# Where the input tiles of a recurrent block start in on-chip memory: shifting them by multiples of 4, 16 and 32 bytes

## The chip, the core and the metric

The kernel runs on one core of a Trainium2 chip. The metric is the device time in microseconds (us) of one execution; lower is better. The kernel before has a median of 2161.11 us over three runs (2160.96 to 2161.13).

## The reference

A two-layer trunk on 1024 tokens of width 1024, in float32: layer 0 mixes tokens with an RG-LRU recurrent block, layer 1 with stick-breaking attention, and each is followed by a SwiGLU feed-forward network (FFN) of width 2816. Norms stand before every part and at the end. The part that matters here is the recurrent block:

```python
def rg_lru_block(x, w_in, b_in, conv_w, conv_b, gate_w, gate_b, lam, w_out, b_out):
    u = jnp.einsum("bsd,de->bse", x, w_in) + b_in          # input product, 1024 -> 2048
    gate_branch, rec = u[..., :LRU_WIDTH], u[..., LRU_WIDTH:]
    rec = causal_depthwise_conv(rec, conv_w, conv_b)
    ...                                                     # block-diagonal gates r and i from rec
    _, h = lax.associative_scan(_linear_recurrence_combine, (a, b), axis=1)
    y = jax.nn.gelu(gate_branch, approximate=True) * h
    return jnp.einsum("bse,ed->bsd", y, w_out) + b_out      # output product, 1024 -> 1024
```

## The kernel before

All activations lie transposed: 128 channels on the partitions, tokens along the free axis, in two halves of 512 tokens (n = 0 left, n = 1 right). A width of 1024 is eight such tiles, d or k = 0 to 7.

A float32 product is made from three matmuls of a reduced type (fp32r). Each operand is split into a high tile and a low tile, its remainder, and `mm3` (L638 to L641) adds high x high, low x high and high x low in one bank of PSUM. The weights are the stationary operand (128 x 128, loaded by LDWEIGHTS); the input is the moving operand (128 x 512). The three matmuls of one k are on L639 (weights high, input high), L640 (weights high, input low) and L641 (weights low, input high). One column of a product, 128 output channels of one half, is eight k, so 24 matmuls.

The moving tiles of the recurrent block are `xh` (high) and `xl` (low), eight of each, a left and a right half for each: 32 tiles of 512 elements, 2048 bytes in each partition. They come from one pool, `xp`, opened by `open_x` (L570). Three pieces of work read them, and a fourth lies between:

- the first four columns of the input product, whose weights `fh` and `fl` are in a pool `sp` of their own (names a_ps<-xh,fh and so on), 192 matmuls, with four small ones for the norm's sums among them;
- the other twelve columns of the input product, 576 matmuls, whose weights `whi` and `wlo` come from a ring of weight tiles of 1024 elements (pools `wp` and `wq`, at the other end of the memory);
- the gates do not read them: their moving tiles `rh` and `rl` are in a pool `lp`, 192 matmuls (g_ps), weights from the ring;
- the output product, 16 columns, 384 matmuls (ob_ps), after the block's result y has been written into the same xh and xl; weights from the ring.

ScalarE writes xh (L758 from the input, L982 from y) and VectorE writes xl as the difference (L761, L983). After the output product the pool is closed, and tiles of the FFN (`vh`, `vl`) are put in its place. From there on other moving tiles are used.

What sets the order: the first part is written out by hand; a planner orders the rest of the recurrent block from its own table of costs, and the FFN again is written out by hand. Every engine works through its own queue; SP's queue issues most of the transfers. Neither the planner nor any of the lists reads an address.

Pools are filled from two ends of the memory of a partition: xp, lp and sp from the low end, one after the other, the ring from the high end. Start addresses of the kernel before, as the program is built, in bytes within a partition:

| tiles | first start | start modulo 256 |
|---|---|---|
| xh, xl (xp, 32 tiles) | 19328 | 128, all |
| fh, fl (sp) | 85248 | 0, all |
| rh, rl (lp) | | 128, all |
| whi, wlo (wp, wq) | 204672 and above | 128, all |
| vh, vl of the FFN | | 128, all |

One k of a weight tile is 512 bytes of it, so within a weight tile the start modulo 256 does not change with k.

Of the kernel before, what the change touches and what calls it, by code (L numbers as in the profile page):

```python
# [10 lines left out]
F32R = mybir.dt.float32r  # L11
# [6 lines left out]
P = 128  # L18
S = 1024
D = 1024  # L20
ND = D // P
NT = S // P
NB = 512
NH = S // NB
# [480 lines left out]
def trunk(  # L505
# [61 lines left out]
    xh, xl = [None] * ND, [None] * ND  # L567
    xstk = ExitStack()

    def open_x():  # L570
        xp = xstk.enter_context(tc.tile_pool(name="xp", bufs=1, reuse_waits="tile"))
        for x_, nm in ((xh, "xh"), (xl, "xl")):
            for d in range(ND):
                x_[d] = [xp.tile([P, NB], F32R, name=f"{nm}{d}_{n}") for n in range(NH)]
    rcol = cp.tile([P, NT], F32, name="rcol")
    minus = cp.tile([P, 112], F32R, name="minus")
    fresh = tiny[:, 60:61]
# [120 lines left out]
    def gain(h, d, n):  # L698
        g = (vc[:, V_FIN : V_FIN + ND], tiny[:, 32 : 32 + ND])[n]
        nc.scalar.activation(h[d][n], h[d][n], AF.Copy, scale=g[:, d : d + 1])  # L700

    open_x()
    hd = [[dp.tile([P, NB], F32, name=f"hd{d}_{n}") for n in range(NH)] for d in range(ND)]
    hstk = ExitStack()
# [1569 lines left out]
```

## Time and profile before

| | us |
|---|---|
| median of the runs | 2161.11 |
| span of the profiled execution, first to last instruction | 2159.4 |
| what lies around the span (2161.11 - 2159.4) | 1.7 |
| TensorE busy | 2148.2 |
| VectorE busy | 1715.8 |
| ScalarE busy | 1099.4 |
| input product with fh, fl | first 52 |
| rest of the input product, and gates | 52 to 226 |
| output product | 226 to 313 |

The profile gives for every instruction its start and its duration. Matmuls are pipelined, so the duration of one (389 ns) contains the time in which the next is running already; what counts for the time is the distance between the starts of one and the next. A group's row names the line, the engine, the operation, and output <- inputs by the names in the program. Times are in us from the start of the span.

### The profile page before, as it was taken

The numbers are of one execution on the slowest core, as the hardware profiler recorded it, in microseconds if no ns is written. First come the engines' busy times: TensorE is split into PE (matmuls) and PEld (weight loads), VectorE is DVE, ScalarE is ACT, GpSimd is POOL, SyncE is SP. The second block draws the span as 40 slices with busy tenths as digits, with TensorE's granted clock in tenths as the row PEclk, the third lists the DMA queues.
The fourth block names the chain that finished last, engine by engine and source line by source line (L and its number), as shares of the span: only waits on it lengthen the run. The fifth ranks groups of instructions, "written<-read, shape, count | busy, mean of one in ns | idle before, by whom it ended". The sixth has DMA issues, their size and how long they took to land.

```text
span 2159.4 us, 27027 instructions
## 1 busy us (share of the span) xinstructions
PE 2148.2 (99%) x9954; PEld 1781.6 (83%) x9954; DVE 1715.8 (79%) x2416; ACT 1099.4 (51%) x1793; POOL 29.2 (1%) x40
## 2 busy tenths in 40 slices
PE   9999999999999999999999999999999999999998
PEld 7888888888888888878888888888888888888887
DVE  8978678667777887888888888877967777787887
ACT  6677445344444544565555555544534444454555
POOL 0000020000000000000000000002000000000000
PEclk9999999999999999999999999999999999999999
DMA  4111312344444764444333334532133444467452
GB/s 177 39 49 49 127 39 84 100 139 146 133 160 136 276 198 122 147 141 103 100 97 96 101 88 107 167 139 95 59 117 125 145 140 151 141 233 243 130 161 86
DMA packets 133316, 274.61 MB, mean 127 GB/s; under 512 B 15296, under 2 KB 23872, under 8 KB 133184
## 3 DMA queue, kind: packets, MB, share of 16 engines
q1 hardware_dynamic: 132768, 272.36, 39.6%
q8 instruction: 78, 1.28, 0.2%
q10 hardware_dynamic: 416, 0.52, 0.1%
q14 instruction: 54, 0.44, 0.1%
HBM read 176.88 MB, written 70.78 MB: 115 GB/s over the span
## 4 chain that ended last, share of the span: by engine, by line
PE 96%; DVE 2%; ACT 1%; issue 0%; DMA 0%; POOL 0%; SPq 0%; DVEq 0%; ACTq 0%; POOLq 0%
PE p_ps L641 18%; PE p_ps L639 18%; PE p_ps L640 18%; PE qk_ps L639 4%; PE qk_ps L641 4%; PE qk_ps L640 4%; PE z_ps L2073 3%; PE av_ps L2121 3%; PE wt_ps L2104 3%; PE a_ps L640 3%; PE a_ps L641 3%; PE a_ps L639 3%; PE ob_ps L639 2%; PE ob_ps L640 2%; PE ob_ps L641 2%; PE g_ps L641 1%
## 5 line engine op out<-in xcount | busy, mean ns | idle before, releaser
L639 PE MATMUL p_ps<-vh,wbh 128*128 128x512 f32 x524 | 204.0, 389 | 1.2 <-ACT ta L1738 1.2
L641 PE MATMUL p_ps<-vh,wal 128*128 128x512 f32 x524 | 204.2, 390 | 0.5 <-DVE wal L1133 0.3
L641 PE MATMUL p_ps<-vh,wbl 128*128 128x512 f32 x524 | 204.1, 390 | 0.0
L641 PE MATMUL p_ps<-vh,wcl 128*128 128x512 f32 x524 | 204.0, 389 | 0.0
L639 PE MATMUL p_ps<-vh,wch 128*128 128x512 f32 x524 | 203.9, 389 | 0.0
L640 PE MATMUL p_ps<-vl,wah 128*128 128x512 f32 x524 | 203.9, 389 | 0.0
L640 PE MATMUL p_ps<-vl,wbh 128*128 128x512 f32 x524 | 203.9, 389 | 0.0
L639 PE MATMUL p_ps<-vh,wah 128*128 128x512 f32 x524 | 203.9, 389 | 0.0
L640 PE MATMUL p_ps<-vl,wch 128*128 128x512 f32 x524 | 203.8, 389 | 0.0
L1138 ACT CAST wbh<-sb 128x1024 fp32r<-128x1024 f32 (+2 forms) x69 | 69.8, 1011 | 191.3 <-DVE sb L1122 191.3
L2085 ACT ACTIVATE F<-z_ps 128x512 f32<-128x512 f32 (+3 forms) x188 | 92.1, 490 | 97.6 <-PE z_ps L2073 95.8
L2109 ACT CAST th<-wt_ps 128x512 fp32r<-128x512 f32 x192 | 92.3, 481 | 84.4 <-PE wt_ps L2104 78.1
L2092 DVE TENSOR_TENSOR_SCAN F<-F,unit 128x128 f32<-128x128 f32 (+3 forms) x128 | 104.9, 821 | 33.4 <-ACT F L2085 32.2
L2113 DVE TENSOR_TENSOR tl<-wt_ps,th 128x512 fp32r<-128x512 f32 x192 | 104.9, 546 | 16.6 <-ACT th L2109 16.5
L641 PEld LDWEIGHTS p_ps<-vh,wal 128*128 128x128 f32 x524 | 98.4, 188 | 22.0 <-DVE wal L1133 1.8
L639 PEld LDWEIGHTS p_ps<-vh,wbh 128*128 128x128 f32 x524 | 98.4, 188 | 21.9 <-ACT ta L1738 1.6
L641 PEld LDWEIGHTS p_ps<-vh,wbl 128*128 128x128 f32 x524 | 98.4, 188 | 21.2 <-DVE wbl L1142 0.8
L641 PEld LDWEIGHTS p_ps<-vh,wcl 128*128 128x128 f32 x524 | 98.4, 188 | 20.7 <-DVE wcl L1152 0.4
L640 PEld LDWEIGHTS p_ps<-vl,wbh 128*128 128x128 f32 x524 | 98.4, 188 | 20.5
L640 PEld LDWEIGHTS p_ps<-vl,wah 128*128 128x128 f32 x524 | 98.4, 188 | 20.5
L639 PEld LDWEIGHTS p_ps<-vh,wch 128*128 128x128 f32 x524 | 98.4, 188 | 20.5
L640 PEld LDWEIGHTS p_ps<-vl,wch 128*128 128x128 f32 x524 | 98.4, 188 | 20.5
(436 smaller groups left out, 5496.4 us busy)
## 6 DMA issues: line engine op xcount, KB each, us to landing
raw<-in_ffn_w_in SPq DMA_DIRECT2D x88, 512.0 KB, 3.6
vl<-pd SPq DMA_DIRECT2D x128, 256.0 KB, 3.5
pd<-U SPq DMA_DIRECT2D x90, 256.0 KB, 2.3
raw<-in_ffn_w_out SPq DMA_DIRECT2D x28, 512.0 KB, 4.1
raw<-in_attn_w_qkv SPq DMA_DIRECT2D x24, 512.0 KB, 3.8
kh<-qh SPq DMA_DIRECT2D x64, 128.0 KB, 2.3
kl<-ql SPq DMA_DIRECT2D x64, 128.0 KB, 2.3
acc<-pd SPq DMA_DIRECT2D x28, 256.0 KB, 2.6
```

The costliest lines, as they stand in the source:

```text
L639: nc.tensor.matmul(ps, lhsT=wh, rhs=mh, start=first, stop=False, **kw)
L640: nc.tensor.matmul(ps, lhsT=wh, rhs=ml, start=False, stop=False, **kw)
L641: nc.tensor.matmul(ps, lhsT=wl, rhs=mh, start=False, stop=last, **kw)
L1138: nc.scalar.copy(self.full(self.wb), self.full(self.sb))
L2073: nc.tensor.matmul(ps[:, 0:n], lhsT=lhsT, rhs=rhs, start=i == 0, stop=i == 1)
L2085: nc.scalar.activation(F, Z.pop(c)[:, 0:n], AF.Sigmoid, scale=-SC)
L2092: V.tensor_tensor_scan(rev, rev, unit[:, NB - n :][:, ::-1], 0.0, op0=ALU.mult, op1=ALU.add)
L2104: nc.tensor.transpose(tp[:, c : c + P], F[:, (kb % 4) * P : (kb % 4 + 1) * P], ident)
L2109: nc.scalar.copy(WH[u][:, c:], TP[u][:, c:])
L2113: V.tensor_sub(WL[u][:, c:], TP.pop(u)[:, c:], f32(WH[u])[:, c:])
L2121: nc.tensor.matmul(ps[:, c:], lhsT=VV[q][:, kb, hx], rhs=t.pop(u)[:, c:], start=kb == 4 * G and i == 0, stop=kb == 3 and i == 1,)
```

## The change

The right halves of xh and xl are taken out of tiles that are 8 elements (32 bytes) longer, and start a few elements into them: 4 elements (16 bytes) for every xh, and 1, 2, 3, 5, 6, 7, 1, 2 elements (4 to 28 bytes) for the eight xl. The left halves start at the start of their tiles. Since each pair is 32 bytes longer, all later tiles of the pool start later too.

```diff
     def open_x():
         xp = xstk.enter_context(tc.tile_pool(name="xp", bufs=1, reuse_waits="tile"))
-        for x_, nm in ((xh, "xh"), (xl, "xl")):
-            for d in range(ND):
-                x_[d] = [xp.tile([P, NB], F32R, name=f"{nm}{d}_{n}") for n in range(NH)]
+        for x_, nm, shifts in ((xh, "xh", (4,) * ND), (xl, "xl", (1, 2, 3, 5, 6, 7, 1, 2))):
+            for d, shift in enumerate(shifts):
+                left = xp.tile([P, NB], F32R, name=f"{nm}{d}_0")
+                x_[d] = [left, xp.tile([P, NB + 8], F32R, name=f"{nm}{d}_1")[:, shift : shift + NB]]
```

In the built program, by start addresses before and after:

| tiles | start after, against before |
|---|---|
| left half of pair p (p = 0 to 7: xh0 to xh7; 8 to 15: xl0 to xl7) | + 32 p bytes |
| right half of an xh | + 32 p + 16 bytes |
| right half of an xl | + 32 p + 4, 8, 12, 20, 24, 28, 4, 8 bytes |
| sp and lp (fh, fl, rh, rl and others) | + 512 bytes |
| the ring, the FFN's tiles, attention's tiles | the same |

The instructions, their shapes and their order on each engine are the same. Of the waits two differ: among the loads of the residual tiles on SP's queue (L714) the wait for VectorE stands at a load three places later, and one of ScalarE's writes of a vh tile of the FFN (L1054), which now lies over two of the old tiles, waits for TensorE.

## The prediction

> **What bounds the kernel now.** I read the page first: busy shares, then the chain of waits.
>
> ```profile
> PE 2148.2 (99%) x9954; PEld 1781.6 (83%) x9954; DVE 1715.8 (79%) x2416; ACT 1099.4 (51%) x1793; POOL 29.2 (1%) x40
> PE 96%; DVE 2%; ACT 1%; issue 0%; DMA 0%; POOL 0%; SPq 0%; DVEq 0%; ACTq 0%; POOLq 0%
> ```
>
> TensorE is busy 99% of the span and holds 96% of the chain, so what changes the pace of its matmuls changes the time one for one. The busy time of one matmul (389 ns) is no pace, since matmuls overlap; the pace is the distance from one start to the next, which I call the step. It comes from first and last starts of the groups that read xh and xl (tile view; the times are first and last start):
>
> ```profile
> L639 PE MATMUL a_ps<-xh,whi x192: 389/389/389, 52.5 to 225.9; 128*128 128x512 f32 x192
> L639 PE MATMUL ob_ps<-xh,whi x128: 389/389/389, 226.6 to 312.9; 128*128 128x512 f32 x128
> L641 PE MATMUL a_ps<-xh,fl x64: 390/394/545, 7.1 to 52.2; 128*128 128x512 f32 x64
> ```
>
> Each group is every third matmul. ob_ps: 127 x 3 = 381 steps in 86.3 us, 226.5 ns each. a_ps from whi: 191 x 3, and the 192 gate matmuls (g_ps) between them, 765 steps in 173.4 us, 226.7 ns. So 960 matmuls on xh and xl (576 of a_ps, 384 of ob_ps) step at 226.7 ns. The 192 first ones, whose weights are fh and fl, take longer: 63 x 3 steps and 4 of the norm sums in 45.1 us, 233.7 ns, a little of it from the start. In order of time, in the middle of that stretch and where it ends:
>
> ```profile
> 19.64 0.40 PE L640 MATMUL a_ps<-xl,fh 128*128 128x512 f32 x1
> 19.88 0.39 PE L641 MATMUL a_ps<-xh,fl 128*128 128x512 f32 x1
> 20.11 0.40 PE L639 MATMUL a_ps<-xh,fh 128*128 128x512 f32 x1
> 20.34 0.39 PE L640 MATMUL a_ps<-xl,fh 128*128 128x512 f32 x1
> ...
> 21.97 0.40 PE L641 MATMUL a_ps<-xh,fl 128*128 128x512 f32 x1
> ...
> 51.76 0.40 PE L639 MATMUL a_ps<-xh,fh 128*128 128x512 f32 x1
> 52.00 0.40 PE L640 MATMUL a_ps<-xl,fh 128*128 128x512 f32 x1
> 52.24 0.40 PE L641 MATMUL a_ps<-xh,fl 128*128 128x512 f32 x1
> 52.47 0.39 PE L639 MATMUL a_ps<-xh,whi 128*128 128x512 f32 x1
> 52.70 0.40 PE L640 MATMUL a_ps<-xl,whi 128*128 128x512 f32 x1
> 52.93 0.39 PE L641 MATMUL a_ps<-xh,wlo 128*128 128x512 f32 x1
> 53.16 0.39 PE L639 MATMUL a_ps<-xh,whi 128*128 128x512 f32 x1
> ...
> 55.88 0.39 PE L639 MATMUL a_ps<-xh,whi 128*128 128x512 f32 x1
> ```
>
> 19.64 to 21.97 is ten steps, 233 ns each. The same xh and xl stand on both sides of 52.47; what changes is the weight tile. From 53.16 to 55.88 are twelve steps, 226.7 ns, and so it stays. In the built programs the xp tiles before the change start 128 bytes past a multiple of 256, the ring tiles (whi, wlo) too; fh and fl start on a multiple of 256. Relative start of weights to moving tile, modulo 256: 0 in the quick stretch, 128 in the slow one.
>
> Two other causes for the slow stretch were open: its loads, and that the kernel is only starting.
>
> ```profile
> 12.00:32.00 20.00, 20.00 (x87) 1.00 0.68 259
> 32.00:52.00 20.00, 20.00 (x87) 1.00 0.12 41
> 60.00:100.00 40.00, 40.00 (x178) 1.00 0.12 40
> ```
>
> These are stretches with TensorE's busy time and matmuls, granted clock, DMA share and GB/s. The count in 20 us is 87 under 259 GB/s and under 41 GB/s; 60 to 100 us, with the DMA share of the second, has 178 in 40 us. The clock is full in all. So the load is not it, and it lasts until the weight tile changes.
>
> The quick step is a state that matmuls fall into, not one that each has for itself. After a wait for a weight tile, in an FFN:
>
> ```profile
> 333.33 0.50 PE L641 MATMUL p_ps<-vh,wal 128*128 128x512 f32 x1
> 333.66 0.40 PE L639 MATMUL p_ps<-vh,wah 128*128 128x512 f32 x1
> 333.90 0.40 PE L640 MATMUL p_ps<-vl,wah 128*128 128x512 f32 x1
> 334.13 0.40 PE L641 MATMUL p_ps<-vh,wal 128*128 128x512 f32 x1
> 334.37 0.39 PE L639 MATMUL p_ps<-vh,wah 128*128 128x512 f32 x1
> 334.59 0.39 PE L640 MATMUL p_ps<-vl,wah 128*128 128x512 f32 x1
> ...
> 335.75 0.39 PE L639 MATMUL p_ps<-vh,wah 128*128 128x512 f32 x1
> ...
> 337.79 0.39 PE L639 MATMUL p_ps<-vh,wah 128*128 128x512 f32 x1
> ```
>
> 333.66 to 335.75 is nine uneven steps (240, 230, 240, 220 ns as rounded), 232 ns on average; from 335.75 nine steps in 2.04 us, 226.7 ns. At 52.47 three steps were enough. With fh and fl nearly 200 steps were not. I take it that the relative start decides whether the even step exists.
>
> **The change part by part.** No instruction is added, removed or moved; sizes and order on every engine are the same. Three things differ.
>
> (1) Starts. Each right tile is 32 bytes longer, so the p-th pair (p = 0 to 15: xh0 to xh7, xl0 to xl7) starts 32p bytes later. Left tiles go to multiples of 32 relative to the ring, right tiles of xh a further 16, right tiles of xl a further 4 to 28. Of 16 left tiles two keep relative start 0 modulo 256 (xh0, xl0) and two get 128 (xh4, xl4); right tiles keep it nowhere. Along a column of eight k the relative start changes after every third matmul. An even step that needs relative start 0 finds it for three matmuls of 24 on the left, where nine were needed after 333.66, and for none on the right. So I let all 960 matmuls lose it. The trace has no step at the new relative starts; the nearest rows are the unsettled ones, 232 ns (5.3 dearer), and those at 128, 233 ns (6.3 dearer). Bounds: 0, if only 128 and what is near it matters, and the longest step seen in the slow stretch, 240 ns as rounded (19.64 to 19.88), 13 dearer. I take 5.5, nearer to the unsettled rows, since changing starts never leave it one pattern. 960 x 5.5 ns = 5.3 us (0 to 12.8).
>
> (2) The gate matmuls (g_ps, 192) have tiles 512 bytes later, so their relative start is the same. They come in some eight stretches between columns and need three to nine steps to settle: 8 x 6 x 5.5 ns = 0.3 us (0 to 1.1, were all 192 unsettled). The FFN after 313 us settles once: under 0.1.
>
> (3) The first 192: fh and fl move by 512 bytes, so their starts against xh and xl become mixed, not 128 throughout. If they settled at 226.7 they would gain 192 x 6.3 = 1.2 us; at 240 they would lose 1.3. Unsettled before and after, I take 0.
>
> ScalarE and VectorE write the shifted tiles.
>
> ```profile
> L758 ACT ACTIVATE xh<-xr,vc x16: 717/722/734, 5.0 to 22.4; 128x512 fp32r<-128x512 f32 x16
> L761 DVE SCALAR_TENSOR_TENSOR xl<-xr,vc,xh x16: 745/747/752, 5.7 to 25.4; 128x512 fp32r<-128x512 f32 x16
> L983 DVE TENSOR_TENSOR xl<-y,xh x16: 665/686/694, 221.5 to 235.7; 128x512 fp32r<-128x512 f32 x16
> ```
>
> Their prices at odd starts are not in the trace; half of each 16 are on right tiles. TensorE covers them: of the first product, columns of the right half start after 96 matmuls, 96 x 233 ns = 22 us after 7.1, so at 29, while the last xl is written by 26.2. In the output product k = 6 and 7 come after 72 matmuls, at 226.6 + 72 x 0.2267 = 242.9, and the last xl ends at 236.4. Without that cover a doubling would cost about 8 x 0.7 us each time; here 0. Two waits move too. On SP's queue the wait for VectorE ahead of the residual loads stands three transfers later, so three loads may go earlier. On ScalarE the first write of a vh6 tile gets a wait for a matmul of the output product:
>
> ```profile
> L1054 ACT ACTIVATE vh<-h,vc x4: 710/713/722, 324.2 to 326.0; 128x512 fp32r<-128x512 f32 x4
> ```
>
> That write is at 324 us or later, the output product is over by 313.5: 0. Behind it on ScalarE are casts for the same FFN, with TensorE supplied from the products before.
>
> The Trainium skill ("SBUF — State Buffer", on cachelines of 16 bytes) has each crossing to a new line cost something. A right xl tile off that grid touches 129 lines, not 128; as an estimate from that page and the step above, 226.7 / 128 = 1.8 ns on 192 matmuls, 0.3 us. The sum would be 0.3 by that alone, and no run here shows it yet.
>
> Sum: 5.3 + 0.3 + 0 = +5.6 us on a span of 2159.4, so 2165.0. The median of the runs, 2161.1, lies 1.7 above that span; the prediction is 2166.7.
>
> **The rivals.**
>
> A (forecast): the even step is lost on xh and xl. Own range from 960 x 3.3 = 3.2 us (all at the 230 ns of the three settling steps from 52.47 to 53.16) to 1152 x 6.3 = 7.3 us: 2164.3 to 2168.4. For it: the switch at 52.47 and nothing else that switches there.
>
> B: nothing happens, 2161.1; not slower. Mechanism: the moving tile and the next weights are read without touching each other, and the first 52 us are slow through what is special to fh and fl themselves (their own start, their narrower tile), which keeps its place modulo 256. For it: only one pool shows the slow pattern. Against: the unsettled steps in the FFN look like it with other tiles. It decides if 60 to 313 us stays at 226.7. The Trainium skill speaks for B: "TensorE: Matmul & The Clock Gate" (Step-by-step) says TensorE has two independent read ports, so that loading the next weights takes nothing from the running matmul; by that rule the time would stay. The step that depends on the weight tile at 52.47 speaks against it.
>
> C: part of it. Only right tiles, off the 32-byte grid, or only those near 128, lose the even step: half of 960, 480 x 5.5 = 2.6 us, 2163.8. For it: no row shows a relative start of 32 or 64.
>
> D: odd starts cost by themselves, an extra piece per read beside the lost step: all 960 at 240 ns or so, 12.8 us, with (2) 2174; half of that extra, 2170. For it only that 240 ns steps occur.
>
> E: faster. A new even step shorter than 226.7. The step from 334.37 to 334.59 shows that 220 ns as rounded occurs; kept for 960 it would give 960 x 6.7 = 6.4 us, 2154.7. Against: it occurs singly and is followed by 230.
>
> **How the numbers follow.** A 0.52, C 0.20, B 0.15, D 0.08, E 0.05. A measurement here tells 0.2% (4.3 us) from no change, so slower begins at 2165.4: some 85% of A (0.45), D (0.08), a little of C (0.02): 0.55. Within: the rest of A, nearly all of C, B, part of E: 0.42. Faster: 0.03. The range goes from 2160.9, which takes in B and C, to 2171.5, which leaves out most of E and about half of D.
>
> **What would show it.** Starts of xh groups: ob_ps's first and last 86.3 us apart now, 88.4 by A, 87.4 by C, unchanged by B. If the columns of the left half stay at 226.7 and only those of the right half lose it, the 32-byte steps were harmless. If the first 52 us grow or shrink by more than 1 us, (3) was wrong. Idle time of TensorE between 52 and 313 us, none now, would mean that a write or a wait was not covered. Wrong altogether if the added time lies after 340 us, where no start changes.

## The result, and the profile after

The changed kernel takes 2166.36 us (median of 10 runs, 2166.07 to 2167.77). The kernel before, on the same chip and between the same runs, takes 2161.19 us (10 runs, 2160.96 to 2161.87). The ratio is 1.0024, with a 95% interval of 1.0014 to 1.0033: slower by 5.2 us. The forecast was 2166.7. The profiled executions stand at spans of 2163.9 and 2159.4 us, 4.5 apart.

The page of the changed kernel, TensorE's share and the chain of waits:

```profile
PE 2152.1 (99%) x9954; PEld 1780.5 (82%) x9954; DVE 1715.6 (79%) x2416; ACT 1098.3 (51%) x1793; POOL 29.0 (1%) x40
PE 95%; DVE 3%; ACT 1%; issue 1%; DMA 0%; SPq 0%; DVEq 0%; ACTq 0%
```

Nothing here tells that anything is wrong: TensorE is busy 99% as before. The kernel got slower without a new wait of any size. The waits of TensorE in the changed kernel begin with these two, one at the start of the kernel and one at 943 us, where the first FFN ends and the attention has not begun:

```profile
PE a_ps L775 <- POOL ident masks.py:199: 1.5, 1, 1.5
PE p_ps L640 <- ACT ta L1739: 1.2, 1, 1.2
```

The same view of the changed kernel between 52 and 313 us has no entry. The loss shows where the first and last starts of a group are read. The tile view of xh in the changed kernel, after the counts the shortest, median and longest duration in ns, then first and last start in us (its lines are one higher than before):

```profile
L640 PE MATMUL a_ps<-xh,whi x192: 387/394/399, 52.1 to 228.4; 128*128 128x512 f32 x192
L640 PE MATMUL ob_ps<-xh,whi x128: 387/395/421, 229.1 to 317.5; 128*128 128x512 f32 x128
L642 PE MATMUL a_ps<-xh,fl x64: 387/393/401, 6.8 to 51.9; 128*128 128x512 f32 x64
L762 DVE SCALAR_TENSOR_TENSOR xl<-xr,vc,xh x16: 745/747/750, 5.7 to 25.6; 128x512 fp32r<-128x512 f32 x16
L984 DVE TENSOR_TENSOR xl<-y,xh x16: 665/684/696, 223.7 to 238.2; 128x512 fp32r<-128x512 f32 x16
```

- a_ps from the ring, with the gates between: 176.3 us from first to last start against 173.4 before, so 2.9 more.
- ob_ps: 88.4 us against 86.3, so 2.1 more: 381 steps of 232.0 ns, where they were 226.5.
- a_ps with fh and fl: 45.1 us, as before.
- The durations say it too. In the even state every matmul of these two groups lasted 389/389/389 ns; now they spread from 387 to 421, with medians of 394 and 395. Here the spread of durations in a group of equal matmuls shows that the even step is gone. It need not spread: in a kernel below whose steps are all 240 ns, 94 of 96 durations are 404 ns.
- VectorE writes xl at the same price as before (747 against 747, 684 against 686 ns), with half of the tiles on odd starts.

The same by stretches, TensorE's busy time, matmuls, granted clock, DMA share and GB/s. First the kernel before (its row for 60 to 100 us stands in the prediction), then the changed one:

```profile
100.00:200.00 100.00, 100.00 (x443) 1.00 0.17 53
230.00:300.00 70.00, 70.00 (x310) 1.00 0.31 105
400.00:800.00 400.00, 400.00 (x1765) 1.00 0.49 164
```

```profile
60.00:100.00 40.00, 40.00 (x175) 1.00 0.13 40
100.00:200.00 100.00, 100.00 (x437) 1.00 0.16 49
230.00:300.00 70.00, 70.00 (x303) 1.00 0.31 106
400.00:800.00 400.00, 400.00 (x1765) 1.00 0.49 162
```

In 70 us of the output product TensorE works on 303 matmuls instead of 310 and is busy for all 70 us in both, at the full clock. From 400 to 800 us, where no start address differs, both have 1765.

### The profile page after: what moved, and what is told of

The parts are those of the page before. It is cut to its first block, busy times and chain, and to the rows that moved or that the text cites. A ratio compares the mean times of both kernels' runs of the same rounds, so it can differ in the third digit from the quotient of the medians.

```text
span 2163.9 us, 27027 instructions
## 1 busy us (share of the span) xinstructions
PE 2152.1 (99%) x9954; PEld 1780.5 (82%) x9954; DVE 1715.6 (79%) x2416; ACT 1098.3 (51%) x1793; POOL 29.0 (1%) x40
## 4 chain that ended last, share of the span: by engine, by line
PE 95%; DVE 3%; ACT 1%; issue 1%; DMA 0%; SPq 0%; DVEq 0%; ACTq 0%
PE p_ps L642 19%; PE p_ps L640 19%; PE p_ps L641 19%; PE qk_ps L640 4%; PE qk_ps L642 4%; PE qk_ps L641 4%; PE z_ps L2074 3%; PE av_ps L2122 3%; PE wt_ps L2105 3%; PE ob_ps L640 2%; PE ob_ps L641 2%; PE ob_ps L642 2%; PE a_ps L642 2%; PE a_ps L640 2%; PE a_ps L641 2%
```

## The experiments

Below, the *step* is the distance from one matmul's start to the next. Means of steps are worked out from all starts that the trace records, with steps above 262 ns (waits) left out. *M* is the start of the moving tile and *W* that of the weights, both modulo 256 bytes; before the change M = 128 for all xh and xl, W = 128 for the ring, W = 0 for fh and fl. "Left" and "right" are the columns of the two halves.

**Which part of the change does it: the 32-byte drift or the fine shifts?** The first kernel keeps the longer tiles and sets every shift to 0:

```diff
-        for x_, nm, shifts in ((xh, "xh", (4,) * ND), (xl, "xl", (1, 2, 3, 5, 6, 7, 1, 2))):
+        for x_, nm, shifts in ((xh, "xh", (0,) * ND), (xl, "xl", (0,) * ND)):
```

> The change without its 4 to 28 byte offsets: the right tiles stay 32 bytes longer, but are used from their start, so all starts lie on a grid of 32 bytes and drift by 32 bytes from pair to pair. If the relative start modulo 256 decides (forecast): left and right columns both stay at 231 to 233 ns a step, about +5 us against before, as the whole change. If the offsets off the 32-byte grid are what costs: 226.7 ns everywhere, 2161.2.

Measured: 2166.75 us (ratio 1.0026, 1.0016 to 1.0035), the same as the whole change. Its output product:

```profile
L640 PE MATMUL ob_ps<-xh,whi x128: 387/395/399, 229.4 to 317.9; 128*128 128x512 f32 x128
```

88.5 us for 381 steps, 232.3 ns; left columns 232.4, right 232.5. The drift alone is enough.

The second kernel does the opposite: left tiles stay where M = W, and the right ones, cut from one row, have the shifts of the change but no drift.

```diff
-                x_[d] = [xp.tile([P, NB], F32R, name=f"{nm}{d}_{n}") for n in range(NH)]
+                x_[d] = [xp.tile([P, NB], F32R, name=f"{nm}{d}_0")]
+        for x_, nm, shifts in ((xh, "xh", (4,) * ND), (xl, "xl", (1, 2, 3, 5, 6, 7, 1, 2))):
+            row = xp.tile([P, ND * NB + 8], F32R, name=f"{nm}r")
+            for i, (shift, d) in enumerate(sorted((s, d) for d, s in enumerate(shifts))):
+                x_[d].append(row[:, i * NB + shift : (i + 1) * NB + shift])
+            xp.tile([P, 56], F32, name=f"pad_{nm}")
```

> The offsets alone: left tiles start as before (relative start 0 modulo 256), right tiles 16 bytes on for xh and 4 to 28 bytes on for xl, with no drift. Left columns 226.7 ns by every theory. If an even step needs relative start 0 exactly: right columns at 231 to 233 ns, half of 960 and of the first 192, about +2.5 us. If a few bytes are within its reach: 226.7 ns, 2161.2. If odd starts have a price of their own: right columns above 233 ns, +3 us or more.

Measured: 2163.72 us (ratio 1.0011, 1.0001 to 1.0020). In its stretches:

```profile
100.00:200.00 100.00, 100.00 (x440) 1.00 0.17 53
230.00:300.00 70.00, 70.00 (x307) 1.00 0.31 106
```

310 before, 303 by the whole change, 307 here. Left columns 227.6 ns (226.7 once settled), right columns 230.9. So the fine shifts are enough as well, for the half that has them. The two parts don't add: the change has both on its right columns, which step at 231.1, no worse than its left ones with the drift alone (232.5).

**Is it the moving tile's own start, or the start relative to the weights?** Here xh and xl stay, with every instruction and wait. A spare tile at the other end of the memory grows by 128 bytes, so the ring and the other tiles at that end begin 128 bytes lower: W = 0 for the ring, M = 128.

```diff
-    edge.tile([P, 24], F32, name="edge")
+    edge.tile([P, 56], F32, name="edge")
```

> The kernel before with the ring of weights, and all that lies at its end of the memory, moved by 128 bytes; xh and xl stay where they were, instructions and waits are the same. If the relative start decides: the recurrent block steps at 232 to 233 ns between 52 and 313 us (1152 matmuls, +7 us) and the FFNs, whose moving tiles lie partly at that end (relative start 0) and partly at the other (128), mix both, some 6300 matmuls at +3 to +5 ns: 2185 to 2200. If the start of the moving tile by itself decides: 2161.2.

Measured: 2189.43 us (ratio 1.0130, 1.0114 to 1.0145), 28 us slower, the largest effect in this study from one number. Stretches:

```profile
100.00:200.00 100.00, 100.00 (x432) 1.00 0.16 48
230.00:300.00 70.00, 70.00 (x303) 1.00 0.32 106
400.00:800.00 400.00, 400.00 (x1737) 1.00 0.48 159
```

303 in the output product, as by the change, though no xh or xl moved (232.4 ns per step). The gates, whose moving tiles did not move either, step at 232.4, and in the FFN, whose columns now mix moving tiles that went along with moving tiles that stayed, the mean step between 400 and 800 us is 230.5 ns where it was 226.7: 1737 matmuls for 1765. So a start that is harmless with one weight tile is slow with another.

This speaks against a rule of the Trainium skill: "TensorE: Matmul & The Clock Gate" (Step-by-step) gives TensorE independent read ports, so that loading the next weights takes nothing from the matmul that runs. Here the place of the weights alone changes the pace of matmuls by 2.5%. What in the chip ties the two together, no run here shows.

**Undoing the slow start of the kernel before.** If fh and fl (W = 0) were 128 bytes on, the first 192 matmuls should find the even step. The first try puts a pad tile into their pool:

```diff
+        sp.tile([P, 32], F32, tag="sppad", name="sppad")
```

> The kernel before with fh and fl moved by 128 bytes, so that the first 192 matmuls have relative start 0 too; nothing else. If the relative start decides: these steps fall from 233 to 226.7 ns, 192 x 6.2 = 1.2 us, 2160.0, faster than both. If the first 52 us are slow for another reason: 2161.2.

Measured: 2171.85 us (ratio 1.0049, 1.0036 to 1.0061), some 10.5 us slower, and not for a reason of steps: the first 192 did settle at 226.7 to 226.9 ns. The waits of VectorE, of ScalarE and of TensorE from 50 to 90 us, each waited for in all, times, longest, and the stretch from 60 to 100:

```profile
DVE u L912 <- PE a_ps L641: 10.0, 1, 10.0
```

```profile
ACT rec L919 <- DVE u L915: 22.7, 2, 14.6
```

```profile
PE g_ps L640 <- DVE rl L968: 6.1, 1, 6.1
```

```profile
60.00:100.00 40.00, 33.03 (x137) 0.91 0.11 35
```

The pad pushed fl7 128 bytes into the place of a later tile u. VectorE's first write of that u now waits 10.0 us for a matmul that reads the old tile; ScalarE's rec waits behind it, and TensorE's first gates wait 6.1 us for rl. 137 matmuls run in 40 us where 178 did. Not all of that is waiting. Behind the wait the gates step at 427 ns for a while, in the stretch whose granted clock is 0.91; from 72.54 to 74.67 are five steps:

```profile
72.54 0.63 PE L639 MATMUL g_ps<-rh,whi 128*128 128x512 f32 x1
...
74.67 0.63 PE L641 MATMUL g_ps<-rh,wlo 128*128 128x512 f32 x1
```

The nine steps from 71.52 to 75.43 take 1.9 us more than nine of 226.7 ns. So the steps of the first 192 matmuls behaved and the time did not: the shift of one pool against another had its own price. In the second try the pad lies in a pool below both sp and lp, so that the two move together and overlap as before; the two U tiles, 64 bytes longer each, bring rh and rl back to their place modulo 256.

```diff
+    lc.tile([P, 32], F32, name="lcpad")
...
-            U[e] = lp.tile([P, S + 16], F32, tag="u", name="u", bufs=2)
+            U[e] = lp.tile([P, S + 32], F32, tag="u", name="u", bufs=2)
```

> Again fh and fl 128 bytes later, but now with the tiles of the pool that comes after them (lp) moved along, so that every wait is the same as in the kernel before; rh and rl keep their start modulo 256. Instructions and waits are those of the kernel before, only start addresses differ. If the relative start decides: first 192 at 226.7 ns as in the run with fh and fl moved alone, and no new wait of VectorE: -1.2 us, 2160.0. If the 8 us lost there came from the starts and not from the wait of VectorE: above 2165.

Measured: 2160.51 us (11 runs, ratio 0.9997, 0.9988 to 1.0005). Its groups:

```profile
L639 PE MATMUL a_ps<-xh,whi x192: 389/389/389, 51.2 to 224.6; 128*128 128x512 f32 x192
L641 PE MATMUL a_ps<-xh,fl x64: 388/389/433, 7.1 to 51.0; 128*128 128x512 f32 x64
```

The first product takes 43.9 us from first to last start where it took 45.1, the durations fall to the 389 of the even state, and the ring begins at 51.2 instead of 52.5. The slow stretch that the kernel before had at its start was a matter of start addresses. The gain is 1.3 us in the trace and 0.7 us in the medians: by the runs it can't be told from no change.

**The curve of the step over the relative start.** Three kernels with constant shifts by multiples of 32 bytes, made with pad tiles ahead of the left and the right tiles; the last pad brings the pools behind back to their place modulo 256.

```diff
-            for d in range(ND):
-                x_[d] = [xp.tile([P, NB], F32R, name=f"{nm}{d}_{n}") for n in range(NH)]
+        xp.tile([P, 16], F32, name="pad0")
+        for n in range(NH):
+            if n:
+                xp.tile([P, 16], F32, name="pad1")
+            for x_, nm in ((xh, "xh"), (xl, "xl")):
+                for d in range(ND):
+                    x_[d] = (x_[d] if n else []) + [xp.tile([P, NB], F32R, name=f"{nm}{d}_{n}")]
+        xp.tile([P, 32], F32, name="pad2")
```

With pads of 16 and 16 elements the left tiles stand 64 bytes on and the right ones 128:

> Constant relative starts: all left tiles 64 bytes on, all right tiles 128 bytes on, weights as before. If relative start 0 is needed: both lose the even step against the ring, +5 us; in the first 192, where the weights are 128 off, the right columns come to 0 and should step at 226.7 ns, -0.6 us; together about 2165.5. If only a change of the relative start from matmul to matmul disturbs: all columns settle at 226.7 ns after some nine steps, 2161 to 2162.

Measured: 2165.04 us (ratio 1.0017, 1.0008 to 1.0026). With pads of 8 and 56, left 32 bytes on and right 256:

> Constant relative starts, left tiles 32 bytes on, right tiles 256 bytes on. If the period is 256 bytes: right columns at 226.7 ns; if it is 512: right columns lost, like a start of their own, 229 to 233. Left at 32: with 64 at 229.4 and 128 at 232.4, a loss that grows with the distance gives some 228; a loss at any distance gives 229 to 232. Total between 2161.8 (228 left, right even) and 2166.

Measured: 2165.43 us (ratio 1.0020, 1.0011 to 1.0029). The right columns come back to the even step, so 256 bytes count as 0, and the other period named, 512, falls; the left ones, at 233.5 ns, are dearer than either guess. With pads of 24 and 24, left 96 and right 192:

> Constant shifts: every left tile 96 bytes on, every right tile 192. Two more points of the curve of step against relative start. Theory (relative start modulo 256, periodic but not known between): ring left (96) and right (192) columns both above 226.7, between 228 and 235; if the curve is symmetric about 128, 192 is as 64, 229.4; if only the lowest set bit counts, 192 is as 64 (229.4) and 96 is as 32 (233.5). Total 2164 to 2166.5 us. Rival (distance to the next multiple of 256 alone, falling): 192 at 227 to 228, 96 between 229.4 and 232.4.

Measured: 2167.70 us in one run, beside 2161.70 for the kernel before, and so above the 2164 to 2166.5 expected: neither guess for 192 bytes held. Each kernel gives the ring's W = 128 and the first product's W = 0, so four of the eight relative starts occur twice, at different places:

| M - W, modulo 256 | with the ring, W = 128 | with fh and fl, W = 0 |
|---|---|---|
| 0 | 226.7 (before, M 128); 226.7 settled (right + 256) | 227.3 with its settling (M 0) |
| 32 | 233.5 (M 160) | |
| 64 | 229.4 (M 192) | 229.1 (M 64) |
| 96 | 233.4 (M 224) | |
| 128 | 232.4 (M 0) | 233.0 (M 128) |
| 160 | | 234.3 (M 160) |
| 192 | 233.1 (M 64) | 233.3 (M 192) |
| 224 | | 233.3 (M 224) |

Mean steps in ns. Where a relative start occurs twice the two agree within 0.6 ns, which is also how far two kernels with the same starts can lie apart (the first product of the kernel whose ring was moved: 232.4 for 233.0). That kernel's ring, at M = 128 and W = 0, has 232.4 as well. In two of the pairs the pattern of single steps is the same: about 226, 229, 232 and again at 64, wherever M is; 231 and 236 in turn at 192. Only 0 and 256 give 226.7. The curve isn't a slope: 64 is the cheapest of the rest, and the distance to the next multiple of 256 doesn't order them. The right columns at + 256 settle after about seven steps (241, 224, 231, 236, 228, 232, 231 in many of them, then 226.7).

In rows, the first product of the kernel with + 64 (left) and + 128 (right), in order of time: 63 steps on the left, 233.3 ns each, and 45 on the right, where M = W = 0, 226.7 ns each.

```profile
9.53 0.40 PE L646 MATMUL a_ps<-xh,fl 128*128 128x512 f32 x1
...
24.23 0.39 PE L646 MATMUL a_ps<-xh,fl 128*128 128x512 f32 x1
...
36.22 0.39 PE L646 MATMUL a_ps<-xh,fl 128*128 128x512 f32 x1
...
46.42 0.39 PE L646 MATMUL a_ps<-xh,fl 128*128 128x512 f32 x1
```

That is the stretch of 233 ns of the kernel before, made even by moving xh and xl and not fh and fl.

**Below 32 bytes.** The tiles of a half are cut from one long row, so that a shift by a few bytes is constant for all of them. Left + 4 bytes, right + 16:

```diff
-            for d in range(ND):
-                x_[d] = [xp.tile([P, NB], F32R, name=f"{nm}{d}_{n}") for n in range(NH)]
+        for n, shift in enumerate((1, 4)):
+            for x_, nm in ((xh, "xh"), (xl, "xl")):
+                row = xp.tile([P, ND * NB + 64], F32R, name=f"{nm}r_{n}")
+                for d in range(ND):
+                    c = d * NB + shift
+                    x_[d] = (x_[d] if n else []) + [row[:, c : c + NB]]
```

> Constant relative starts, left tiles 4 bytes on, right tiles 16 bytes on, all xh and xl. If a few bytes off the start lose the even step: left and right at 229 to 232 ns, +2.5 to +5 us. If it was the change of start from xh to xl and from k to k that lost it on the right side in the run with the offsets alone: 226.7 ns in both, 2161.2. A price of 4 byte starts as such (a further piece to read) would show as a left step above 226.7 that is the same in each matmul.

Measured: 2169.29 us (ratio 1.0038, 1.0024 to 1.0052), with the dearest steps of the study. In the first product 63 steps on the left take 240.0 ns each, all of them alike; 45 on the right 233.3:

```profile
9.60 0.40 PE L644 MATMUL a_ps<-xhr,fl 128*128 128x512 f32 x1
...
24.72 0.40 PE L644 MATMUL a_ps<-xhr,fl 128*128 128x512 f32 x1
...
36.04 0.39 PE L643 MATMUL a_ps<-xlr,fh 128*128 128x512 f32 x1
...
46.54 0.39 PE L643 MATMUL a_ps<-xlr,fh 128*128 128x512 f32 x1
```

With the ring the left columns step at 237.4 and the right ones at 231.8. If only the relative start counted, moving fh and fl by 4 bytes as well should give the even step on the left:

```diff
-        fh = [one(f"fh{k}", F32R) for k in range(ND)]
-        fl = [one(f"fl{k}", F32R) for k in range(ND)]
...
+        wide = lambda name: sp.tile([P, NB + 64], F32R, tag=name, name=name)[:, 33 : 33 + NB]
+        fh = [wide(f"fh{k}") for k in range(ND)]
+        fl = [wide(f"fl{k}") for k in range(ND)]
```

> Constant shifts of 4 bytes (left tiles) and 16 bytes (right tiles) as in the run with +4 and +16, but the weights of the first 192 matmuls (fh, fl) now also begin 132 bytes on, so that for the left columns of this first stretch both operands stand on a start that is 4 bytes off and their relative start is 0 modulo 256; for the right columns the relative start becomes 12. The program's pieces in the working pool stand closer, so later waits may differ; only the steps of the matmuls are read. Theory (only the relative start counts): first 192, left columns at 226.7 ns, right columns above it, 229 to 240; ring columns as in the run with +4 and +16, left 237.4 and right 231.8. Rival (a start off the 16-byte grid costs by itself): first 192, left columns stay near 240.

```profile
9.55 0.40 PE L644 MATMUL a_ps<-xhr,fl 128*128 128x512 f32 x1
...
24.53 0.40 PE L644 MATMUL a_ps<-xhr,fl 128*128 128x512 f32 x1
...
36.12 0.40 PE L642 MATMUL a_ps<-xhr,fh 128*128 128x512 f32 x1
...
46.33 0.39 PE L642 MATMUL a_ps<-xhr,fh 128*128 128x512 f32 x1
```

The theory fell twice. On the left, M = W = 132, relative start 0, and 63 steps take 237.8 ns each. On the right, M = 144 and W = 132, relative start 12, and 45 steps take 226.9: the even step, where it was not expected. (One run: 2168.96 us, beside 2161.70.)

So below 32 bytes the moving tile's own start might count. Two more kernels of the same make ask that: left 0, right + 8, with W = 132 for fh and fl; and left + 12, right + 16, with W = 144.

> Left tiles unshifted, right tiles a constant 8 bytes on; the weights of the first 192 matmuls (fh, fl) begin 132 bytes on, 4 bytes past the left tiles modulo 256. The run with both operands 4 bytes off a 128-byte boundary left its first columns at 237.6 ns, so relative start 0 is not enough. Theory now (the moving tile's own start counts beside the relative one: a start off the 16-byte grid costs some 11 ns wherever the weights are): ring left 226.7, ring right (moving 8 off) 236 to 241; first 192, left (moving on 128, weights 4 past it) 226.7 to 233, right (moving 8 off) 236 to 241. Rival (only the relative start counts, and 0 there was an exception): ring right anything between 228 and 235, first 192 left near 237, as with 4 bytes between them elsewhere.

> Left tiles a constant 12 bytes on, right tiles 16; the weights of the first 192 matmuls begin 144 bytes on, so that on the right both operands are 16 bytes past 128 (relative start 0). Theory (a moving start off the 16-byte grid costs by itself; on that grid the relative start decides): ring left 236 to 241, ring right 231.8 as measured for +16; first 192, left 236 to 241, right 226.7. Rival (relative start alone): first 192, right 226.7 too, but the 12-byte columns anywhere from 228 to 235. Rival (the moving tile's distance from a 128-byte boundary alone): first 192, right as in the ring, 231.8.

The first product of the former (2166.34 us in one run) and then of the latter (2165.26), rows as above:

```profile
9.54 0.40 PE L642 MATMUL a_ps<-xhr,fh 128*128 128x512 f32 x1
...
24.18 0.40 PE L642 MATMUL a_ps<-xhr,fh 128*128 128x512 f32 x1
...
36.28 0.40 PE L642 MATMUL a_ps<-xhr,fh 128*128 128x512 f32 x1
...
46.81 0.39 PE L642 MATMUL a_ps<-xhr,fh 128*128 128x512 f32 x1
```

```profile
9.54 0.39 PE L644 MATMUL a_ps<-xhr,fl 128*128 128x512 f32 x1
...
24.04 0.39 PE L644 MATMUL a_ps<-xhr,fl 128*128 128x512 f32 x1
...
36.05 0.39 PE L644 MATMUL a_ps<-xhr,fl 128*128 128x512 f32 x1
...
46.45 0.39 PE L644 MATMUL a_ps<-xhr,fl 128*128 128x512 f32 x1
```

232.4 (left) and 234.0 (right); 230.2 (left) and 231.1 (right). All of it together, mean steps in ns:

| M | W = 0 | W = 128 | W = 132 | W = 144 |
|---|---|---|---|---|
| 128 | 233.0 | 226.7 | 232.4 | |
| 132 | 240.0 | 237.4 | 237.6 | |
| 136 | | 232.8 | 233.8 | |
| 140 | | 229.3 | | 230.0 |
| 144 | 233.4 | 231.8, 231.3 | 227.2 with its settling | 231.2 |

No rule of one number fits. That a start off the 16-byte grid costs 11 ns by itself, as the last two texts had it, holds at + 4 (237 to 240 whatever W is) and fails at + 8 and + 12 (229 to 234). The relative start alone fails at M = W = 132 and 144. The moving tile's own start alone fails in the rows of 128 and 144, where W makes 6 ns. What these runs carry: with every moving tile on a multiple of 32 bytes, and weights at 0 or 128 (the only places of theirs that were tried there), the relative start modulo 256 decides; below that both starts matter, and how is left open. The two theories were not tried on the xl tiles one by one; in the mixed columns of the change and of the kernel with the fine shifts alone the step of a single matmul depends on its neighbours, and their means (231.1 and 230.9) lie below those of the constant + 4.

## Why the prediction was right, and where it was not

**Step 1, the 960 matmuls on xh and xl: right, and near in size.** Forecast 960 x 5.5 = 5.3 us for the loss of the even step. The steps went from 226.7 to 231.8 ns on average (left 232.5, right 231.1): 960 x 5.1 = 4.9 us, of which the groups' rows show 2.9 us in a_ps (with the gates) and 2.1 in ob_ps. First to last start of ob_ps is 88.4 us, the figure named for the forecast; the case in which only the right half loses had 87.4 and no change 86.3. That the price came out near is in part luck. It was taken from rows of 232 ns in which matmuls settle at relative start 0, and those say nothing of other starts; the runs with constant shifts show that each start has a step of its own, 229.1 to 234.3 ns at the seven other multiples of 32. The mean of the eight values of the table, 232.0 as an estimate, is near the 232.4 that the drift gives, and near 232 by chance only. One reading was too short: the relative start changes after every third matmul only on the left; on the right xh and xl have different shifts, so it changes with every matmul. The reason given, relative start modulo 256, holds for the drift of 32 bytes and is shown by the run that moved the weights only. For the fine shifts it is incomplete: relative start 0 on 4- or 16-byte places did not give the even step.

**Step 2, the gates: right in kind, small.** Forecast 0.3 us. Their steps averaged 227.2 ns after 226.7: 192 x 0.5 = 0.1 us. In the FFN nothing is lost: 1765 matmuls from 400 to 800 us in both.

**Step 3, the first 192: 0 forecast, a gain of 0.4 us measured.** The ring begins at 52.1 instead of 52.5. About 0.1 of it lies before the first of these matmuls (a start 4.18 us after the first matmul of all, 4.30 before), and 0.4 in the first three steps (1.40 us for 1.76). The steps behind them, 231.7 ns on average for 233.0, give 0.2 more, and TensorE loses 0.3 of it around the four matmuls of the norm sums (1.27 us for 0.94). So only the 0.2 can belong to the starts, and half of that is what two kernels with the same starts can differ by. The 0.4 is within the bounds given (1.2 less to 1.3 more). The kernel that put all 192 on relative start 0 shows that the bound of a gain was a fair one: 1.3 us.

**The writers and the waits: 0, as forecast.** The prediction covered the writers' unknown prices by TensorE's work; it turned out that there is nothing to cover, for xl costs 747 and 684 ns (747 and 686 before) and xh 716 (722 before). No wait entered between 52 and 313 us, and after 317 nothing is added: the last matmul of ob_ps's xh group is 4.6 us later than before and the end of the span 4.5.

Sum in the trace: 2.9 + 2.1 - 0.4 = 4.6 us, against 5.6 forecast. The runs' medians are 5.2 apart, 0.7 more than the spans. That is the choice of executions: in the runs whose span is on record the time of these two kernels lies 2.2 to 2.3 us above it, so the profiled execution of the kernel before, at 2159.4, is one of some 2161.7 us, 0.5 above its median, and that of the changed kernel took 2166.20, 0.2 below its own. The 1.7 us that the prediction added to the span is therefore not what lies around an execution. The forecast doesn't suffer, since span and 1.7 together are the median before.

**The rivals.** That nothing happens is refuted by 303 matmuls for 310, and the rule of the Trainium skill that spoke for it ("TensorE: Matmul & The Clock Gate", Step-by-step) does not give the time here. That shifts by multiples of 32 bytes are harmless and only the right half loses: refuted, the drift alone gives 2166.75. Odd starts that cost by themselves: not in this change, whose right columns with odd starts are no dearer than its left ones; at a constant + 4 they do, with 240.0 ns, the price that this rival had. The estimate from "SBUF — State Buffer" of the Trainium skill, 1.8 ns for one more line at an odd start, is not borne out either way: + 12 cost 2.6 ns with the ring, + 4 cost 10.7, and by that page of the Trainium skill both touch one line more. A faster step than 226.7 as a mean was in no run.

## What to carry to other kernels

Where matmuls run one behind the other with new weights each time (here 128 x 128 by 128 x 512 in fp32r, the only form tried), put the moving tiles and the weight tiles on the same start modulo 256 bytes. Both at 0 and both at 128 gave the even step, both at 132 and both at 144 did not, and other equal starts were not tried. Look for it in the distance of starts of a group of equal matmuls, since busy shares and waits do not show it. It is worth 1 to 3% of such a stretch here for shifts by 32 bytes and up, but in a kernel that is bound by TensorE that is all of it: one pad of 128 bytes under the weights costs 28 us of 2161. When a tile is moved to mend it, look at what shares its memory first, since a tile that reaches 128 bytes further brought waits, and slow matmuls behind them, that cost eight times what the shift gained in the trace.

## What the runs showed of the hardware that was not expected

- Some columns settle on one step and keep it for dozens of matmuls: 226.7, 233.3 and 240.0 ns, 6.67 apart, and 230.0 with left + 12 in the first product; others repeat a pattern (226, 229, 232; 231 and 236 in turn; 234, 240, 240).
- The step over the relative start isn't monotonous: 229.3 ns at 64 bytes, but 233.5 at 32 and 233.2 at 192.
- M = 144 with W = 132 (12 bytes apart) settles on the same even step as M = W = 128. This one is unexplained.
- The kernel that had a wait of 6.1 us had a granted clock of 0.91 in the stretch from 60 to 100 us, while all others show 1.00 there, and its steps right behind that wait are 427 ns.
- VectorE's writes of xl, half of them on odd starts, cost what they cost before (747 ns).
